# GELU of a state-space unit as one ScalarE activation instead of a five-step tanh form, in a Hymba block whose inverse square roots are powers on GpSimd

## The chip, the cores and the metric

One core of one Trainium2 chip runs the whole block. The time is the device time of one execution in microseconds (us). Two kernels are compared by the medians of their runs; the profile is of one more execution, whose own time is given beside its span.

## The reference

The input is 2048 positions of 1024 channels in float32; 16 learned meta tokens are put in front. One layer is computed:

```python
n1 = rmsnorm(h, norm1_g)
proj = n1 @ w_in                       # 1024 -> 1024
u = proj[..., :512]                    # 32 groups x 16 channels
v = proj[..., 512:]                    # 4 groups x 128 channels
# S5: 64 complex states a group, s[t] = a*s[t-1] + b u[t]
y = Re(C s) + d * u
g = jax.nn.gelu(y)                     # the tanh form
ys = g * sigmoid(g @ glu_w + glu_b)    # per group
# pooling: trailing means over 2, 4, 8, 16 positions minus v,
# then a 128x128 map per group
mixed = concat(rmsnorm(ys), rmsnorm(yp))
h = h + mixed @ w_out
ff = silu(n2 @ w_gate) * (n2 @ w_up)   # n2 = rmsnorm(h), 1024 -> 2816
h = h + ff @ w_down
out = rmsnorm(h)[16:]
```

The GELU is the step that the change touches; its tanh form is y/2 * (1 + tanh(0.798 * (y + 0.0447 y^3))).

## The kernel before

All large products are float32 by three matmuls on split operands: a high part h, rounded to the matmul's format, and the rest l, with hh + hl + lh (mm3, L119 to L121). So each weight and each activation that is multiplied is split first: the high part (names ending in h) on ScalarE (L112, or L115 with a scale), the low part (names ending in l) on VectorE (L87, or L96 with a scale).

The 2048 positions are cut into two halves, b = 0 and 1, of 1024: 128 chunks of T = 8 positions. The state space works on chunks: a unit is 4 of the 32 groups, so there are eight units a half, and ssm_unit(b, u) (L657 on) does one:

- pk, the unit's constants, comes by DMA (L661). For every second unit the projected input xu is turned to channel-major, by PE transposes into put (L669) and ScalarE copies to us (L670).
- pvs (L686, PE) is what the chunk adds to the state. VectorE rotates it (wr, tmp), scans it over the chunks (L691, z), and rotates back to st, with two products tmp on GpSimd; the step st<-st,tmp on VectorE is the last. In half 0 some small instructions on 128 x 4 elements (carry, sm) carry the state from half to half and start it from the meta tokens (pv, L677 and L678).
- py (PE, one bank of PSUM, 128 x 512): L700 is the part straight from us, L701 the part from the states st.
- The GELU of py goes to yview, which is the tile xu of that half. ScalarE squares py (L703), VectorE makes q = (q + 1) py, ScalarE the tanh (L705), and VectorE four times (q + 1) py, one instruction per group with a permuted write; all of VectorE's are the helper's line L96. The result is twice the GELU, and the factor is taken back later: in the tanh of the gate (L786, scale 0.25) and in the eps of the norm (L815, 16 EPS).

In time, the kernel runs through these stages. Up to 165 us are weights, parameters and the projection of half 0. Then the projection of half 1 (pj) runs on PE with the units of half 0 between its slices, to 296 us. In the transition, the eight tiles of w_out are loaded into two raw buffers (wraw) and split into wh and wl (load_w). The output stage then goes through eight position slots of half 0: out_pool transforms the pooled channels (pin, ppool), out_ssm turns g to position-major (pg, copied to gt, L780), multiplies by the gate's weights (pgate, L783), makes the gate with tanh (th, L786) and the product gt, and sums squares (sq, sqs on GpSimd); out_mm adds the norms' sums (pss, L812) and the output projection (po). Between the slots stand the units of half 1 and pool_block(1), which makes the trailing means with adds on GpSimd (sum), one VectorE instruction (pt) and a write to p_d1 by DMA. The output stage of half 1 follows to 560 us and the FFN after it.

The program is written in this order, but the order in which an engine's queue gets its instructions is chosen by a scheduler, at build time, from its own estimates of cost. At run time each engine runs its queue in that order; SyncE's queue issues the DMAs. PSUM tiles come from three pools; py, pvs and pv share the one with two buffers (ps_s).

Of the kernel before, what the change touches and what calls it, by code (L numbers as in the profile page):

```python
# [9 lines left out]
F32 = mybir.dt.float32  # L10
# [3 lines left out]
AF = mybir.ActivationFunctionType  # L14
ALU = mybir.AluOpType

P = 128
# [3 lines left out]
DSSM = 512  # L21
G = 32
H = 16
S = 64
T = 8
NB = 2
NCH = 128
UG = 4
# [1 line left out]
FF = 2816  # L30
NF = FF // P
EPS = 1e-6
GA = 0.7978845608028654
GC = math.sqrt(0.044715)
MAGIC = 12582912.0
PKN = 2568

# [2 lines left out]
def kernel(  # L40
# [54 lines left out]
    def stt(o, a, s, b, op0, op1):  # L95
        V.scalar_tensor_tensor(o, a, s, b, op0=op0, op1=op1)  # L96
# [560 lines left out]
    def ssm_unit(b, u):  # L657
        g0 = u * UG
        gs = slice(g0, g0 + UG)
        pk = ss_p.tile([P, PKN], F32, name="pk", tag="pk", bufs=2)  # L660
        SY.dma_start(pk, pk_d[u])  # L661
        pm, nm, mm = g4(pk[:, :512]), g4(pk[:, 512:1024]), g4(pk[:, 1024:1536])
        ct, sg = g4(pk[:, 1536:2052]), g4(pk[:, 2052:2568])
        if u % 2 == 0:
            us8[0] = ss_p.tile([P, 2 * UG, NCH], F32, name="us", tag="us", bufs=2)
            for h in range(2):
                pu = tr_tile("put")
                for i in range(UG):
                    PE.transpose(pu[:, i], xu[b][:, g0 + h * UG + i].rearrange("c t h -> c (t h)"), ident)  # L669
                A.copy(us8[0][:, h * UG:(h + 1) * UG], pu)  # L670
        us = us8[0][:, (u % 2) * UG:(u % 2 + 1) * UG]
        z = ss_p.tile([P, UG, NCH + 1], F32, name="z", tag="z", bufs=2)
        sm = ss_p.tile([P, 4, UG], F32, name="sm", tag="sm", bufs=2)
        if b == 0:
            pv0 = g4(s_tile("pv0"))
            for i in range(UG):
                PE.matmul(pv0[:, i, :2], pm[:, i], um_sb[:, g0 + i], start=True, stop=True)  # L677
            V.tensor_copy(sm[:, 2:4], pv0[:, :, :2].rearrange("p g c -> p c g"))  # L678
            rotate(sm[:, 0], sm[:, 1], sm[:, 2], ct[:, :, 1], sg[:, :, 1], 1)
            tt(sm[:, 0], sm[:, 0], r8[:, gs], M_)  # L680
            tt(z[:, :, 0], sm[:, 0], sm[:, 3], A_)
        else:
            V.tensor_copy(z[:, :, 0], carry[:, gs])
        pv = g4(s_tile("pvs"))
        for i in range(UG):
            PE.matmul(pv[:, i], pm[:, i], us[:, i], start=True, stop=True)  # L686
        wr = ss_p.tile([P, UG, NCH], F32, name="wr", tag="wr")
        tmp = ss_p.tile([P, UG, NCH], F32, name="tmp", tag="tmp", bufs=2)
        rotate(wr, tmp, pv, ct[:, :, 1:], sg[:, :, 1:], -1)
        for i in range(UG):  # L690
            V.tensor_tensor_scan(z[:, i, 1:], r8[:, g0 + i:g0 + i + 1].to_broadcast([P, NCH]), wr[:, i],  # L691
                                 z[:, i, 0:1], op0=M_, op1=A_)
        st = ss_p.tile([P, UG, NCH], F32, name="st", tag="st")
        tmp2 = ss_p.tile([P, UG, NCH], F32, name="tmp2", tag="tmp", bufs=2)
        rotate(st, tmp2, z[:, :, :NCH], ct[:, :, :NCH], sg[:, :, :NCH], 1, GP)
        if b == 0:
            rotate(carry[:, gs], sm[:, 1], z[:, :, NCH], ct[:, :, NCH], sg[:, :, NCH], 1)
        py = s_tile("py")
        for i in range(UG):
            PE.matmul(py[:, i * P:(i + 1) * P], us[:, i], mm[:, i], start=True, stop=False)  # L700
            PE.matmul(py[:, i * P:(i + 1) * P], st[:, i], nm[:, i], start=False, stop=True)  # L701
        q = ss_p.tile([P, UG * P], F32, name="q", tag="q")
        A.activation(q, py, AF.Square, scale=GC)  # L703
        stt(q, q, 1.0, py, A_, M_)
        A.activation(q, q, AF.Tanh, scale=GA)  # L705
        yv = yview(b)[:, u // 2]
        for i in range(UG):
            c0 = (u % 2 * UG + i) * H
            isl = slice(i * P, (i + 1) * P)
            stt(yv[:, :, c0:c0 + H], q[:, isl].rearrange("c (t h) -> c t h", h=H), 1.0,  # L710
                py[:, isl].rearrange("c (t h) -> c t h", h=H), A_, M_)

    def pool_block(b):
        vt = vts.pop(b)
# [59 lines left out]
    def out_ssm(b, t, mh, ml, sq):  # L774

        pt = tr_tile("pg")
        for k in range(4):
            PE.transpose(pt[:, k], yview(b)[:, k, t], ident)
        gt = wo_p.tile([P, 4, NCH], F32, name="gt", tag="gt")
        A.copy(gt, pt)  # L780
        pg = (s_tile if b else mm_tile)("pgate")
        for k in range(4):
            PE.matmul(pg[:, k * P:(k + 1) * P], glubd[:, k], gt[:, k], start=True, stop=True)  # L783
        th = wo_p.tile([P, 4, NCH], F32, name="th", tag="th")
        for k in range(4):
            A.activation(th[:, k], pg[:, k * P:(k + 1) * P], AF.Tanh, scale=0.25, bias=halfb[:, k:k + 1])  # L786
        fl = "p k c -> p (k c)"
        stt(gt.rearrange(fl), th.rearrange(fl), 1.0, gt.rearrange(fl), A_, M_)
        split(mh[:, :4], ml[:, :4], gt)
        A.activation(sq[:, 0], gt, AF.Square)  # L790
        tt(sq[:, :, :2], sq[:, :, :2], sq[:, :, 2:], A_, GP)
        sqs = wo_p.tile([P, 2, NCH], F32, name="sqs", tag="sqs", bufs=2)
        tt(sqs, sq[:, :, 0], sq[:, :, 1], A_, GP)
        return mh, ml, sqs
# [12 lines left out]
    def out_mm(b, t, mh, ml, sq, pooled=None):  # L807
        hx = hxs.pop((b, t))
        os = [None, pooled or out_half(mh, ml, 1)]
        pss = tr_tile("pss")  # L810
        for i in range(2):
            PE.matmul(pss[:, 0, i:i + 1], sq[:, i], ones, start=True, stop=True)  # L812
        rsp = small.tile([P, 2], F32, name="rsp", tag="rsp")
        rsqrt_into(rsp, pss[:, 0, :2], [2],
                   [((ALL[0], slice(0, 1)), 1.0 / DSSM, 16.0 * EPS),  # L815
                    ((ALL[0], slice(1, 2)), 1.0 / DSSM, EPS)])
        os[0] = out_half(mh, ml, 0)
        for q in (1, 0):
            for h in range(2):
                cs2 = slice(h * 512, (h + 1) * 512)  # L820
                stt(hx[:, cs2], os[q][h], rsp[:, q:q + 1], hx[:, cs2], M_, A_)
        for h in range(2):
            cs2 = slice(h * 512, (h + 1) * 512)
            jk = wo_p.tile([P, 4, NCH], F32, name="jk", tag="th")
            A.activation(jk.rearrange("p k c -> p (k c)"), hx[:, cs2], AF.Square, accum_out=ss2[:, h, b * T + t:b * T + t + 1])
        SY.dma_start(h2_d[b][t], hx)
        if t == T - 1:
            bs = slice(b * T, b * T + T)
            tt(ss2[:, 0, bs], ss2[:, 0, bs], ss2[:, 1, bs], A_)
            rsqrt_into(rs2[:, bs], ss2[:, 0, bs], [T], [(ALL, 1.0 / D, EPS)])  # L830
# [433 lines left out]
```

## Time and profile before

| what | value |
|---|---|
| median of three runs | 1892.83 us (1889.36 to 1895.19) |
| profiled execution, its own time | 1896.96 us |
| its span | 1895.2 us |
| TensorE busy | 1827.5 us |
| VectorE busy | 1250.3 us |
| GpSimd busy | 814.5 us |
| ScalarE busy | 681.9 us |

The span runs from the first to the last instruction of the profile; the rest of the execution's time lies around it. A row of a view names source line, engine, operation, and the tile written and the tiles read. PE is TensorE's matmuls, PEld its weight loads, DVE VectorE, ACT ScalarE, POOL GpSimd, SP SyncE. In brackets stands how long the engine was idle before the instruction and what ended that. Lines L87, L93, L96, L112 and L115 are those of helpers, and such rows are known by their tiles.

### The profile page before, as it was taken

Reading aid. Unit: us, or ns where it says so; the run is one execution under the profiler, and the core shown is the slowest. Engines: PE = TensorE matmul, PEld = TensorE weight load, DVE = VectorE, ACT = ScalarE, POOL = GpSimd, SP = SyncE. Lnnn points to the kernel's source line nnn. Section 1 sums busy time; section 2 is a strip of 40 time slices with the busy share of each in tenths; the row PEclk is TensorE's granted clock in tenths of the full one; section 3 lists DMA queues with packets and bytes.
Section 4 is the critical chain, followed back from the end, with each engine's and each line's share of the span. In section 5 each row is a group of like instructions: output and inputs, shape, how many; then the busy total and the mean of one; then the engine's idle time right before and its main releaser. Section 6 shows DMA issues by size and latency. Waiting matters only on the chain.

```text
span 1895.2 us, 23776 instructions
## 1 busy us (share of the span) xinstructions
PE 1827.5 (96%) x8497; PEld 1499.8 (79%) x8497; DVE 1250.3 (66%) x1993; ACT 681.9 (36%) x1228; POOL 814.5 (43%) x619
## 2 busy tenths in 40 slices
PE   7989996899999999999999999999999999999998
PEld 5867785788887788888887788888888888888886
DVE  5985878966456866666667866766666344435763
ACT  4332334343454333333335333233323343333441
POOL 1774424633244564554646866666562000003400
PEclk9999998899999999999999999999999999999999
DMA  6254425444355343543426654455447765536761
GB/s 181 69 176 164 137 92 172 172 156 137 102 177 162 114 159 106 169 139 125 156 95 202 200 197 139 156 170 172 130 150 228 213 202 177 153 102 208 249 215 71
DMA packets 260519, 298.38 MB, mean 157 GB/s; under 512 B 17148, under 2 KB 204048, under 8 KB 255536
## 3 DMA queue, kind: packets, MB, share of 16 engines
q1 hardware_dynamic: 260304, 296.84, 49.2%
q8 instruction: 67, 1.10, 0.2%
q14 instruction: 52, 0.43, 0.1%
q0 software_dynamic: 96, 0.01, 0.0%
HBM read 202.37 MB, written 96.53 MB: 158 GB/s over the span
## 4 chain that ended last, share of the span: by engine, by line
PE 73%; DVE 2%; DMA 2%; POOL 1%; ACT 1%; issue 1%; DVEq 0%; POOLq 0%; ACTq 0%
PE pr L119 14%; PE pr L120 14%; PE pr L121 14%; PE pd L119 8%; PE pd L120 7%; PE pd L121 7%; PE po L119 2%; PE po L121 2%; PE po L120 2%; DMA xp<-xr_d 1%; PE ptx L874 1%; PE pgate L783 1%; DMA hr<-h_d 1%; DVE wcl L87 1%; PE ppool L769 0%
## 5 line engine op out<-in xcount | busy, mean ns | idle before, releaser
L112 ACT CAST wch<-raw 128x512 fp32r<-128x512 f32 x176 | 108.6, 621 | 266.1 <-PE pr L120 240.0
L87 DVE TENSOR_TENSOR wcl<-raw,wch 128x512 fp32r<-128x512 f32 x176 | 178.0, 1014 | 37.7 <-ACT wch L112 36.7
L87 DVE TENSOR_TENSOR fl<-fr,fh 128x512 fp32r<-128x512 f32 x168 | 116.0, 702 | 127.5 <-ACT fh L112 120.7
L112 ACT CAST fh<-fr 128x512 fp32r<-128x512 f32 x168 | 96.5, 584 | 212.8 <-PE pd L120 180.0
L112 ACT CAST wch<-s 128x512 fp32r<-128x512 f32 x132 | 82.0, 622 | 228.2 <-PE pr L120 175.2
L87 POOL TENSOR_TENSOR s<-raw 128x512 f32<-128x512 f32 x44 | 67.7, 1540 | 173.3 <-DVE wcl L87 72.3
L87 DVE TENSOR_TENSOR wcl<-s,wch 128x512 fp32r<-128x512 f32 x132 | 117.6, 892 | 20.5 <-ACT wch L112 20.2
L87 POOL TENSOR_TENSOR db22h<-db22h,hd 128x512 f32<-128x512 f32 x4 | 5.2, 1291 | 256.4 <-DVE db22h L87 256.4
L87 POOL TENSOR_TENSOR rs<-rv,mhalf 128x1 f32<-128x1 f32 (+2 forms) x35 | 40.6, 1160 | 154.9 <-DVE rv L93 151.8
L119 PE MATMUL po<-wh,mh 128*128 128x512 f32 x256 | 104.4, 408 | 1.5 <-DVE hx L96 0.8
L119 PE MATMUL pj<-wh,xh 128*128 128x512 f32 x256 | 102.5, 408 | 3.2 <-ACT xh L112 2.3
L120 PE MATMUL pj<-wl,xh 128*128 128x512 f32 x256 | 102.9, 404 | 0.0
L121 PE MATMUL pj<-wh,xl 128*128 128x512 f32 x256 | 102.3, 405 | 0.0
L120 PE MATMUL po<-wl,mh 128*128 128x512 f32 x256 | 101.3, 396 | 0.0
L121 PE MATMUL po<-wh,ml 128*128 128x512 f32 x256 | 100.9, 395 | 0.0
L87 POOL TENSOR_TENSOR wr<-wr 128x512 f32<-128x512 f32 x44 | 67.3, 1530 | 72.9 <-DMA wr<-in_w_down_dram 67.8
L87 DVE TENSOR_TENSOR gt<-gt,ut 128x512 f32<-128x512 f32 x88 | 94.0, 1069 | 0.0
L87 POOL TENSOR_TENSOR tmp<-z,pk 64x512 f32<-64x512 f32 x32 | 49.7, 1553 | 84.3 <-issue 82.4
L87 DVE TENSOR_TENSOR gt<-pr,gt 128x512 f32<-128x512 f32 x66 | 45.4, 690 | 58.6 <-PE pr L121 58.4
L87 POOL TENSOR_TENSOR ut<-gt 128x512 f32<-128x512 f32 x22 | 33.4, 1520 | 107.7 <-DVE gt L87 107.7
L119 PE MATMUL pr<-xt2h,wch 128*128 128x512 f32 x176 | 69.9, 397 | 6.1 <-DVE gt L87 3.7
L1015 ACT ACTIVATE gt<-gt 128x512 f32<-128x512 f32 x88 | 55.5, 632 | 49.8 <-DVE gt L87 49.6
(394 smaller groups left out, 5611.2 us busy)
## 6 DMA issues: line engine op xcount, KB each, us to landing
fr<-ff_d SPq DMA_DIRECT2D x56, 704.0 KB, 5.0
raw<-in_w_gate_dram SPq DMA_DIRECT2D x44, 512.0 KB, 4.8
raw<-in_w_up_dram SPq DMA_DIRECT2D x44, 512.0 KB, 4.2
ff_d<-gt SPq DMA_DIRECT2D x22, 1024.0 KB, 3.9
pk<-pk_d SPq DMA_DIRECT2D x16, 1284.0 KB, 6.0
ff_d<-ut SPq DMA_DIRECT2D x22, 768.0 KB, 5.6
wr<-in_w_down_dram SPq DMA_DIRECT2D x22, 512.0 KB, 3.3
wd_d<-wr SPq DMA_DIRECT2D x22, 512.0 KB, 3.4
```

The source lines that it names most:

```text
L87: e.tensor_tensor(o, a, b, op=op)
L112: A.copy(hi, src)
L119: PE.matmul(o, lh, rh, start=first, stop=False)
L120: PE.matmul(o, lh, rl, start=False, stop=False)
L121: PE.matmul(o, ll, rh, start=False, stop=last)
L783: PE.matmul(pg[:, k * P:(k + 1) * P], glubd[:, k], gt[:, k], start=True, stop=True)
L874: PE.transpose(pt[:, k], r[:, (4 * h + k) * P:(4 * h + k + 1) * P], ident)
L1015: lambda i, j: A.activation(gt[:, i, j], gt[:, i, j], AF.Silu), b == 0 and f0 == 0)
```

## The change

The square, the two kinds of VectorE instruction and the tanh give way to one activation, Gelu_apprx_tanh, that reads py and writes yview permuted. Since the result is now the GELU and not twice it, the gate's tanh is scaled by 0.5 and the eps is 4 EPS.

```diff
@@ -30,8 +30,6 @@
 FF = 2816
 NF = FF // P
 EPS = 1e-6
-GA = 0.7978845608028654
-GC = math.sqrt(0.044715)
 MAGIC = 12582912.0
 PKN = 2568
 
@@ -699,16 +697,9 @@
         for i in range(UG):
             PE.matmul(py[:, i * P:(i + 1) * P], us[:, i], mm[:, i], start=True, stop=False)
             PE.matmul(py[:, i * P:(i + 1) * P], st[:, i], nm[:, i], start=False, stop=True)
-        q = ss_p.tile([P, UG * P], F32, name="q", tag="q")
-        A.activation(q, py, AF.Square, scale=GC)
-        stt(q, q, 1.0, py, A_, M_)
-        A.activation(q, q, AF.Tanh, scale=GA)
-        yv = yview(b)[:, u // 2]
-        for i in range(UG):
-            c0 = (u % 2 * UG + i) * H
-            isl = slice(i * P, (i + 1) * P)
-            stt(yv[:, :, c0:c0 + H], q[:, isl].rearrange("c (t h) -> c t h", h=H), 1.0,
-                py[:, isl].rearrange("c (t h) -> c t h", h=H), A_, M_)
+        c0 = u % 2 * UG * H
+        yv = yview(b)[:, u // 2][:, :, c0:c0 + UG * H].rearrange("c t (i h) -> c t i h", h=H)
+        A.activation(yv, py.rearrange("c (i t h) -> c t i h", i=UG, t=T), AF.Gelu_apprx_tanh)
 
     def pool_block(b):
         vt = vts.pop(b)
@@ -783,7 +774,7 @@
             PE.matmul(pg[:, k * P:(k + 1) * P], glubd[:, k], gt[:, k], start=True, stop=True)
         th = wo_p.tile([P, 4, NCH], F32, name="th", tag="th")
         for k in range(4):
-            A.activation(th[:, k], pg[:, k * P:(k + 1) * P], AF.Tanh, scale=0.25, bias=halfb[:, k:k + 1])
+            A.activation(th[:, k], pg[:, k * P:(k + 1) * P], AF.Tanh, scale=0.5, bias=halfb[:, k:k + 1])
         fl = "p k c -> p (k c)"
         stt(gt.rearrange(fl), th.rearrange(fl), 1.0, gt.rearrange(fl), A_, M_)
         split(mh[:, :4], ml[:, :4], gt)
@@ -812,7 +803,7 @@
             PE.matmul(pss[:, 0, i:i + 1], sq[:, i], ones, start=True, stop=True)
         rsp = small.tile([P, 2], F32, name="rsp", tag="rsp")
         rsqrt_into(rsp, pss[:, 0, :2], [2],
-                   [((ALL[0], slice(0, 1)), 1.0 / DSSM, 16.0 * EPS),
+                   [((ALL[0], slice(0, 1)), 1.0 / DSSM, 4.0 * EPS),
                     ((ALL[0], slice(1, 2)), 1.0 / DSSM, EPS)])
         os[0] = out_half(mh, ml, 0)
         for q in (1, 0):
```

Source lines after the change are 2 lower up to py and 9 lower from pool_block on: L703 and L705 are replaced by L702. On ScalarE there is one table load more than before, ahead of the first GELU; before, and after, one stands at the start and one at the FFN's first SiLU. The scheduler puts instructions in another order from the first GELU, about 186 us, to about 470 us; the rest of the queues, the FFN's among them, is as it was.

VectorE in the projection of half 1, around the end of unit (0,1): its rotation step is st<-st,tmp, and the instructions on 128x4 and 64x4 from sm on belong to the next unit. Before:

```order
L93 TENSOR_SCALAR rv<-ss 128x1
L678 COPY sm<-pv_2095 128x8
L87 TENSOR_TENSOR sm<-sm,pk 128x4
L87 TENSOR_TENSOR sm<-sm,pk 64x4 x2
L87 TENSOR_TENSOR sm<-sm 128x4
L87 TENSOR_TENSOR sm<-sm,r_156 128x4
L87 TENSOR_TENSOR z<-sm 128x4
L87 TENSOR_TENSOR st<-st,tmp_1968 128x512
```

and now:

```order
L85 TENSOR_TENSOR xl<-pt,xh 128x512
L91 TENSOR_SCALAR rv<-ss 128x1
L676 COPY sm<-pv_2081 128x8
L85 TENSOR_TENSOR st<-st,tmp_1961 128x512
L85 TENSOR_TENSOR sm<-sm,pk 128x4
L85 TENSOR_TENSOR sm<-sm,pk 64x4 x2
L85 TENSOR_TENSOR sm<-sm 128x4
L85 TENSOR_TENSOR sm<-sm,r_156 128x4
L85 TENSOR_TENSOR z<-sm 128x4
L94 SCALAR_TENSOR_TENSOR pt<-sum_1836,vt_495 128x8x128
L85 TENSOR_TENSOR wr<-pvs,pk 128x512
```

The step st<-st,tmp has moved ahead of the next unit's sm instructions, and pt of pool_block(0) now stands between these and that unit's wr.

VectorE at the end of the projection, around the end of unit (0,7); wl are splits of w_out, pt is of pool_block(1), wr and tmp from pvs are those of unit (1,0). Before:

```order
L87 TENSOR_TENSOR carry<-z,pk 128x4
L87 TENSOR_TENSOR sm<-z,pk 64x4 x2
L96 SCALAR_TENSOR_TENSOR wl_3003<-wraw,vcol,wh_3002 128x1024
L87 TENSOR_TENSOR carry<-carry,sm 128x4
L96 SCALAR_TENSOR_TENSOR wl_3009<-wraw,vcol,wh_3008 128x1024
L87 TENSOR_TENSOR st<-st,tmp_2852 128x512
L683 COPY z<-carry 128x4
L96 SCALAR_TENSOR_TENSOR wl_3015<-wraw,vcol,wh_3014 128x1024
L96 SCALAR_TENSOR_TENSOR q<-q,py 128x512
L96 SCALAR_TENSOR_TENSOR wl_3021<-wraw,vcol,wh_3020 128x1024
```

and now:

```order
L85 TENSOR_TENSOR sm<-z,pk 64x4 x2
L85 TENSOR_TENSOR carry<-carry,sm 128x4
L85 TENSOR_TENSOR st<-st,tmp_2803 128x512
L681 COPY z<-carry 128x4
L94 SCALAR_TENSOR_TENSOR wl_2947<-wraw,vcol,wh_2946 128x1024
L94 SCALAR_TENSOR_TENSOR wl_2953<-wraw,vcol,wh_2952 128x1024
L94 SCALAR_TENSOR_TENSOR wl_2959<-wraw,vcol,wh_2958 128x1024
L85 TENSOR_TENSOR wr<-pvs,pk 128x512
L85 TENSOR_TENSOR tmp<-pvs,pk 64x512 x2
L94 SCALAR_TENSOR_TENSOR pt<-sum_3107,vt_2031 128x8x128
L94 SCALAR_TENSOR_TENSOR wl_2965<-wraw,vcol,wh_2964 128x1024
```

The step st<-st,tmp has moved ahead of the first two splits, the third split has stayed ahead of unit (1,0)'s wr, and the two kinds of GELU instruction are gone. On PE, the matmuls that read this st (L701, now L699) have moved from behind the last matmul of the projection to sixteen matmuls ahead of it.

ScalarE at the same place; wh are the high parts of w_out, xu and vs the projected last slice, vt the transposed vs, us and gt copies of put and pg. Before:

```order
L219 ACTIVATE xu_160<-pj,rs 128x32x16
L226 ACTIVATE vs<-pj,rs 128x512
L115 ACTIVATE wh_3014<-wraw,vcol 128x1024
L703 ACTIVATE q<-py 128x512
L115 ACTIVATE wh_3020<-wraw,vcol 128x1024
L230 COPY vt_2045<-ptv 128x4x128
L705 ACTIVATE q<-q 128x512
L670 COPY us<-put 128x512 x2
L780 COPY gt<-pg 128x512
```

and now:

```order
L702 ACTIVATE xu_159<-py 128x8x64
L113 ACTIVATE wh_2952<-wraw,vcol 128x1024
L217 ACTIVATE xu_160<-pj,rs 128x32x16
L224 ACTIVATE vs<-pj,rs 128x512
L228 COPY vt_2031<-ptv 128x4x128
L771 COPY gt<-pg 128x512
L668 COPY us<-put 128x512
L113 ACTIVATE wh_2958<-wraw,vcol 128x1024
L668 COPY us<-put 128x512
L113 ACTIVATE wh_2964<-wraw,vcol 128x1024
```

The copy to vt has moved from behind the third and fourth of these wh to a place ahead of the third.

SyncE's queue issued the last six of w_out's eight tiles in three pairs, the second pair ahead of the first write of p_d1 and the third ahead of the second write. Now a pair and a single tile stand ahead of the first write of p_d1, a pair between the two writes, and the last tile behind the second.

## The prediction

> **What bounds the kernel now.** I read the page first: its first part (busy time by engine) and the slices.
>
> ```profile
> PE 1827.5 (96%) x8497; PEld 1499.8 (79%) x8497; DVE 1250.3 (66%) x1993; ACT 681.9 (36%) x1228; POOL 814.5 (43%) x619
> PE   7989996899999999999999999999999999999998
> PEclk9999998899999999999999999999999999999999
> ```
>
> TensorE is busy 96% of the span, and the change takes no matmul away. It can only shorten the time in which PE stands idle, or runs at a reduced granted clock. A slice is 47.4 us; besides the start, PE's digit falls in the seventh and eighth, at 284 to 379 us, and the clock with it. Next I asked for the stretches by engine (stretch and length; busy PE, PEld, DVE, ACT, POOL; granted clock; DMA share; GB/s).
>
> ```profile
> 165.00:460.00 295.00, 264.47 (x1503) 229.35 (x1502) 232.26 (x441) 106.33 (x209) 131.05 (x102) 0.95 0.40 137
> 296.00:336.00 40.00, 24.84 (x138) 22.13 (x139) 33.41 (x43) 16.23 (x27) 24.22 (x16) 0.79 0.55 177
> 313.00:336.00 23.00, 15.40 (x86) 13.91 (x86) 22.94 (x27) 9.21 (x17) 19.32 (x12) 0.78 0.41 125
> 560.00:1895.20 1335.20, 1319.11 (x5751) 1070.68 (x5749) 842.88 (x1101) 468.74 (x810) 567.35 (x389) 1.00 0.52 163
> ```
>
> From 560 us on is the FFN, whose order stays. The sixteen state-space units lie in 165 to 460 us, where PE idles 295.0 - 264.5 = 30.5 us. That is all the change can win there, beside the clock. Half of it, 40.0 - 24.8 = 15.2 us, lies in the 40 us between the projection and the full run of the output projection; I call it the transition. The waits of PE in 165 to 460 us name what ends them (total us, times, longest):
>
> ```profile
> PE py L701 <- DVE st L87: 12.0, 6, 3.0
> PE pss L812 <- POOL sqs L87: 4.7, 2, 3.8
> PE put L669 <- ACT vt L230: 2.9, 1, 2.9
> PE pvs L686 <- DVE sm L678: 2.5, 1, 2.5
> ```
>
> PE waits for st, the rotated states, which VectorE makes: for a VectorE queue that the GELU shares, not for the GELU itself. The timeline gives each wait its place (start, length, instruction, and in brackets the idle time before it):
>
> ```profile
> 183.42 0.49 PE L686 MATMUL pvs<-us,pk 128*128 128x128 f32 x2 [2.46 <-DVE sm L678]
> 185.24 0.63 PE L700 MATMUL py<-pk,us 128*128 128x128 f32 x2
> 206.63 0.49 PE L701 MATMUL py<-pk,st 128*128 128x128 f32 x2 [2.98 <-DVE st L87]
> 206.96 0.39 PE L700 MATMUL py<-pk,us 128*128 128x128 f32 x2
> 295.47 0.39 PE L121 MATMUL pj<-wh,xl 128*128 128x512 f32 x1
> 298.90 0.49 PE L701 MATMUL py<-pk,st 128*128 128x128 f32 x2 [3.04 <-DVE st L87]
> 304.44 1.12 PE L669 MATMUL put<-ident,xu 128*128 128x128 f32 x4 [2.95 <-ACT vt L230]
> 327.51 1.01 PE L812 MATMUL pss<-ones,sqs 128*128 128x1 f32 x4 [3.75 <-POOL sqs L87]
> 335.65 0.49 PE L119 MATMUL po<-wh,mh 128*128 128x512 f32 x1
> ```
>
> **Removed and added work.** The groups of instructions (busy total, mean ns of one, idle before):
>
> ```profile
> L703 ACT ACTIVATE q<-py 128x512 f32<-128x512 f32 x16 | 9.5, 591 | 35.4 <-PE py L701 32.9 <-issue 2.5
> L705 ACT ACTIVATE q<-q 128x512 f32<-128x512 f32 x16 | 10.1, 634 | 11.3 <-DVE q L96 11.2
> L96 DVE SCALAR_TENSOR_TENSOR q<-q,py 128x512 f32<-128x512 f32 x16 | 10.9, 684 | 10.2 <-ACT q L703 10.1
> L96 DVE SCALAR_TENSOR_TENSOR xu<-q,py 128x128 f32<-128x128 f32 x64 | 14.0, 279 | 2.2 <-ACT q L705 2.2
> L219 ACT ACTIVATE xu<-pj,rs 128x512 f32<-128x512 f32 x16 | 11.0, 687 | 16.3 <-PE pj L121 14.4 <-POOL ptp L87 1.8
> ```
>
> VectorE loses 10.9 + 14.0 = 24.9 us in 80 instructions, 1.56 us a unit; ScalarE loses 9.5 + 10.1 = 19.6 us. It gains sixteen GELUs that read py in PSUM and write permuted. No row shows one. Nearest are L703, the same read (591 ns), and L219, which reads PSUM and writes the same tile xu permuted (687 ns): 9.5 to 11.0 us in all. I take 0.6 us each, by L703, since in L219 the scale is a tile. Either way ScalarE ends 8.6 to 10.1 us lighter, at 36% busy, so the GELU itself is at nothing. If a reader of it came early, the price would be 0.1 us a unit. The new scales of L786 and the eps of L815 change no instruction: nothing.
>
> A table load is added at the first GELU. Its price is in the FFN's switch to SiLU:
>
> ```profile
> 598.07 1.28 ACT L1015 ACT_TABLE_LOAD   x1
> 599.37 0.63 ACT L1015 ACTIVATE gt<-gt 128x512 f32<-128x512 f32 x1
> 187.19 0.60 ACT L703 ACTIVATE q<-py 128x512 f32<-128x512 f32 x1 [11.49 <-PE py L701]
> ```
>
> From the load's start to the next ACTIVATE pass 1.30 us. The first GELU is where L703 stands at 187.19, and ScalarE idled 11.49 us in front of it: hidden. Without that cover it would cost 1.3. The Trainium skill (ScalarE: Activation LUTs, section "What ACT_TABLE_LOAD costs") counts 2.66 us for a switch, a load of 1283 ns and a drain of 1380 ns. The trace agrees on the load and shows no drain behind it; by the skill's figure the uncovered cost would be 2.7 instead of 1.3, and the sum the same.
>
> **Unit 1, the wait at 206.63.** VectorE's rows ahead of it:
>
> ```profile
> 204.78 1.20 DVE L87 TENSOR_TENSOR z<-sm 128x4 f32<-128x4 f32 x1
> 205.90 0.68 DVE L87 TENSOR_TENSOR st<-st,tmp 128x512 f32<-128x512 f32 x1
> ```
>
> The last rotation step of st stands behind the sm chain of unit 2, tiny instructions that the busy GpSimd stretches (1.20 us for 4 columns). In the new order it stands ahead of the chain, and PE loses the 2.98 us no more: bounds 0 to -3.0. What is late next: the chain is now followed by pt, which waits for a GpSimd sum, ahead of unit 2's wr, so unit 2 may be held. I give 1.0 back: -2.0. The 2.46 at 183.42 lies before the first changed VectorE instruction and stays.
>
> **The transition.** Before, two w_out splits stand ahead of st of unit (0,7); vt, the transposed v for which PE's put waits, stands on ScalarE behind splits that wait for a DMA.
>
> ```profile
> 296.97 1.28 DVE L96 SCALAR_TENSOR_TENSOR wl<-wraw,vcol,wh 128x1024 fp32r<-128x1024 f32 x1
> 298.16 0.68 DVE L87 TENSOR_TENSOR st<-st,tmp 128x512 f32<-128x512 f32 x1
> 302.77 1.15 ACT L115 ACTIVATE wh<-wraw,vcol 128x1024 fp32r<-128x1024 f32 x1 [0.83 <-DMA wraw<-in_w_out_dram]
> 303.83 0.56 ACT L230 COPY vt<-ptv 128x512 f32<-128x512 f32 x1
> 324.59 2.28 DVE L96 SCALAR_TENSOR_TENSOR wl<-wraw,vcol,wh 128x1024 fp32r<-128x1024 f32 x1
> 327.93 2.28 DVE L87 TENSOR_TENSOR st<-st,tmp 128x512 f32<-128x512 f32 x1
> 331.02 2.87 DVE L96 SCALAR_TENSOR_TENSOR wl<-wraw,vcol,wh 128x1024 fp32r<-128x1024 f32 x1
> ```
>
> After, st goes ahead of the splits and 2 x 1.28 = 2.6 us of them drop out of its chain, with 1.56 us of the previous unit's GELU; its matmuls move from behind the projection's last matmul to 16 ahead of it, so that these sixteen cover the rest. So the 3.04 goes. vt no longer follows the third and fourth wh: the 2.95 goes. Then the limit is the w_out splits. The last, 331.02 + 2.87 = 333.9, is followed by the po run at 335.65, 335.65 - 295.86 = 39.8 us after the projection's last matmul. VectorE's queue until 333.9 held 33.4 less about 2 us behind it, 31.4, and loses 1.56: last split at the earliest 30 us after. If nothing is stretched there (the last two splits took 2.28 and 2.87 instead of 1.28, the st at 327.93 took 2.28 instead of 0.68: 4.2 us), 26. With 2 us behind it, the po run starts 28 to 32 us after instead of 39.8: -7.8 to -11.8. I take the middle, -9.8, less 0.3 for the third split, which now stands ahead of unit (1,0)'s wr and needs a load: -9.5. It contains the 3.75 before pss and the reduced clock (0.79 over the stretch), not twice. The bound above is 0, if the splits' loads, not VectorE, set their end (rivals).
>
> **Later units.** Of the 12.0 us for st, 3.0 + 3.0 are spent above; the rest is partly in the transition. Out of the window's last 124 us I take -0.5 (0 to -4).
>
> Sum: -2.0 - 9.5 - 0.5 = -12.0. The profiled execution took 1896.96 us (span 1895.2), so 1885; it lies 4.1 above the median 1892.83, so **1881**.
>
> The Trainium skill (TensorE: Matmul & The Clock Gate, section "Part 1: The HAM clock gate") says that the clock halves after an idle window of about 3.4 us. Here pairs of matmuls took 0.63 us (185.24) behind the 2.46 us wait and 0.39 (206.96) behind the 2.98 one, so the trace does not follow the length of a single wait. Had the rule held at unit 1, its removed wait would win some 1.7 us more (an estimate from that page: 3.4 us at half clock); by the rows it wins nothing more.
>
> **The rivals.**
>
> *The waits come back elsewhere (no change).* The removed instructions all lie outside 313 to 336 us, where VectorE is busy 22.94 of 23.0; PE may just reach that block sooner and wait in it. For: that row. Against: st and vt feed the block. It gives -2.0 for unit 1 and -2 of the transition: 1889.
>
> *The loads become the bound (slower).* SyncE's queue now issues the last six raw tiles as two, one, two and one instead of in three pairs, the last one behind the second write of p_d1, which waits for VectorE's pt and GpSimd's sums. Three rounds become four.
>
> ```profile
> 297.00 1.60 SPq L204 DMA_DIRECT2D wraw<-in_w_out_dram  x2
> ```
>
> The other view, DMA issues (count, size, median us to landing):
>
> ```profile
> wraw<-in_w_out_dram SPq DMA_DIRECT2D x8, 512.0 KB, 3.3
> ```
>
> A round is landing 3.3 us, wh 1.15, wl 1.28 to 2.87, and the wait for the queue; before, three rounds took 333.9 - 297.0 = 36.9, 12.3 each. A fourth like them ends at +12.3; with unit 1's -2.0 that is +10.3: 1903. It decides from the point where the last split ends more than 38 us after the projection. Against: a bare round is 3.3 + 1.15 + 1.28 = 5.7, and four are 23 us.
>
> *The one activation is not one (no change to slower).* If the tables alternate between GELU and the gate's Tanh, eight units of half 1 bring 16 loads of 1.30: 20.8 us on ScalarE, at most all on the path from pgate to th, 1881 + 20.8 = 1902. The Trainium skill (ScalarE: Activation LUTs, section "Table sets: the hidden batching unit") tells to group functions by set, and lists gelu's set as separate from gelu_apprx_tanh. Against: the order holds one added load.
>
> *All waits go (faster).* PE's idle 30.5, less the 2.46 that stays and 3 of mixed small ones, is 25, and 1892.8 - 25 = 1868.
>
> **How the numbers follow.** Forecast (1875 to 1887) 0.61, all waits 0.08, no change 0.19, loads 0.10, tables 0.02. About 0.3% (5.7 us) can be told from no change: faster is below 1887.2, slower above 1898.5. Faster takes the forecast and all waits, 0.69; same 0.19; slower 0.12. The range reaches from 1868 to 1893, past the no-change case by its 4 us of spread, and leaves the loads and tables out.
>
> **What would show it.** Right: L702 at 0.6 to 0.7 us; no wait above 1 us for st near 205 us nor at the projection's end; no put wait for vt; the po run 27 to 32 us after the projection's last matmul; PE idle 18 to 20 us in 165 to 460. Wrong: that po run 38 us or more after it, wh waiting for wraw in front of it, or table loads between GELU and Tanh.

## The result, and the profile after

The changed kernel took 1885.98 us (median of 13 runs, 1882.54 to 1888.96); the kernel before, beside it, 1895.19 us (13 runs, 1889.07 to 1899.9). The ratio is 0.995, 95% interval 0.994 to 0.996: 9.2 us faster. The profiled execution took 1885.98 us, its span is 1884.2.

The page of the changed kernel, first part and slices:

```profile
PE 1822.9 (97%) x8497; PEld 1495.4 (79%) x8497; DVE 1232.4 (65%) x1913; ACT 673.8 (36%) x1213; POOL 816.9 (43%) x619
PE   7989997899999999999999999999999999999998
PEclk9999998999999999999999999999999999999999
```

PE's busy time itself fell by 4.6 us although it runs the same 8497 matmuls. VectorE lost 17.9 us, not 24.9: 7 us came back, since instructions that remain took longer.

The stage borders are read from PE's timeline: the first pv of half 0 (up to there the instructions are the same), the end of the projection's last matmul, and the first matmul of the FFN (pr; it starts at 587.99 us before and 577.91 after, so the output stage of half 1 reaches to there and not to 560 us). The stretches between them, as windows, first of before and then of after (stretch and length; busy PE, PEld, DVE, ACT, POOL; granted clock; DMA share; GB/s):

```profile
166.44:295.86 129.42, 123.06 (x706) 106.20 (x706) 105.44 (x229) 42.58 (x72) 52.06 (x42) 0.99 0.34 118
295.86:587.99 292.13, 265.82 (x1459) 229.11 (x1459) 193.29 (x317) 121.99 (x275) 125.25 (x102) 0.95 0.47 154
```

```profile
164.43:295.76 131.33, 125.12 (x720) 107.25 (x720) 99.89 (x198) 40.66 (x67) 51.15 (x42) 0.99 0.35 122
295.76:577.91 282.15, 259.67 (x1446) 222.97 (x1445) 182.28 (x267) 116.01 (x265) 129.32 (x102) 0.97 0.47 157
```

The projection has become 1.9 us longer, but it holds 14 more matmuls, which came forward from behind it; its idle time is 6.4 us before and 6.2 now. The stretch behind it is 10.0 us shorter: 3.8 us less idle (26.3 to 22.5) and 6.2 us less busy, 2.1 of them the matmuls that moved. So in the two stretches together idle time fell by 4.0 and busy time, at a higher granted clock (0.97 instead of 0.95 in the second), by 4.1.

The waits of PE in 165 to 460 us, after:

```profile
PE py L698 <- DVE tmp L85: 8.6, 1, 8.6
PE pvs L684 <- DVE sm L676: 5.8, 2, 3.4
PE pgate L774 <- ACT gt L771: 3.6, 4, 1.2
PE put L667 <- ACT gt L771: 3.5, 1, 3.5
PE py L699 <- DVE st L85: 1.2, 3, 0.8
PE put L667 <- ACT vt L228: 0.2, 1, 0.2
```

The 12.0 us for st are 1.2, and the 2.9 for vt are 0.2, as the order foretold. In their place the wait for tmp has grown from 2.1 us to 8.6, that of pvs from 2.5 to 5.8, and one of 3.5 for gt is new. The wait for tmp before:

```profile
PE py L700 <- DVE tmp L87: 2.1, 1, 2.1
```

In time (PE, after):

```profile
198.93 0.49 PE L699 MATMUL py<-pk,st 128*128 128x128 f32 x2 [0.25 <-DVE st L85]
213.65 1.35 PE L684 MATMUL pvs<-us,pk 128*128 128x128 f32 x8 [3.38 <-DVE sm L676]
295.37 0.39 PE L119 MATMUL pj<-wh,xl 128*128 128x512 f32 x1
297.93 1.15 PE L667 MATMUL put<-ident,xu 128*128 128x128 f32 x8 [0.24 <-ACT vt L228]
304.27 1.05 PE L774 MATMUL pgate<-gt,glubd 128*128 128x128 f32 x8
321.35 0.77 PE L698 MATMUL py<-pk,us 128*128 128x128 f32 x2 [8.59 <-DVE tmp L85]
323.35 2.08 PE L774 MATMUL pgate<-gt,glubd 128*128 128x128 f32 x8 [1.23 <-ACT gt L771]
328.45 0.48 PE L117 MATMUL po<-wh,mh 128*128 128x512 f32 x1
```

The last row is the start of the po run. VectorE's last split ends behind it, at 327.43 + 1.75 = 329.18:

```profile
327.43 1.75 DVE L94 SCALAR_TENSOR_TENSOR wl<-wraw,vcol,wh 128x1024 fp32r<-128x1024 f32 x1
```

The eight pgate matmuls of a slot take 1.05 us before the long wait and 2.08 behind it. The GELU itself, and its table load:

```profile
L702 ACT ACTIVATE xu<-py 128x512 f32<-128x512 f32 x16 | 9.4, 590 | 25.2 <-PE py L699 25.2
```

```profile
173.74 1.28 ACT L702 ACT_TABLE_LOAD   x1
183.93 0.60 ACT L702 ACTIVATE xu<-py 128x512 f32<-128x512 f32 x1 [8.91 <-PE py L699]
```

590 ns, at the low end of the bounds, permuted write or not; the load lies in ScalarE's idle time, and there is no other between GELU and tanh.

### The profile page after: what moved, and what is told of

It reads as the page before. It is cut to its first block, busy times and chain, and to the rows that moved or that the text cites. A ratio compares the mean times of both kernels' runs of the same rounds, so it can differ in the third digit from the quotient of the medians.

```text
span 1884.2 us, 23676 instructions
## 1 busy us (share of the span) xinstructions
PE 1822.9 (97%) x8497; PEld 1495.4 (79%) x8497; DVE 1232.4 (65%) x1913; ACT 673.8 (36%) x1213; POOL 816.9 (43%) x619
## 4 chain that ended last, share of the span: by engine, by line
PE 73%; DVE 3%; DMA 2%; POOL 1%; issue 1%; ACT 1%; DVEq 0%; POOLq 0%; ACTq 0%
PE pr L117 14%; PE pr L118 14%; PE pr L119 14%; PE pd L117 8%; PE pd L118 8%; PE pd L119 8%; PE po L117 2%; PE po L119 2%; PE po L118 2%; DVE wcl L85 1%; PE pgate L774 1%; DMA hr<-h_d 1%; PE ptx L865 1%; DMA xp<-xr_d 0%; PE ppool L760 0%
## 5 line engine op out<-in xcount | busy, mean ns | idle before, releaser
L85 POOL TENSOR_TENSOR rs<-rv,mhalf 128x1 f32<-128x1 f32 (+2 forms) x35 | 31.5, 900 | 154.1 <-DVE rv L91 144.8
```

The source lines that it names most:

```text
L85: e.tensor_tensor(o, a, b, op=op)
```

## The experiments

Theory A: the gain is VectorE's queue, lighter and in another order. Its rival, theory B: the gain is the shorter way from py to the GELU. A second rival within A: the order alone, not the work. Each time is the median beside runs of the kernel before on the same chip; "faster" and "slower" are against those.

**One half at a time.** One half takes the one activation and the other keeps the five steps (here half 0; in the other kernel b == 1):

```diff
+        if b == 0:
+            c0 = u % 2 * UG * H
+            yv = yview(b)[:, u // 2][:, :, c0:c0 + UG * H].rearrange("c t (i h) -> c t i h", h=H)
+            A.activation(yv, py.rearrange("c (i t h) -> c t i h", i=UG, t=T), AF.Gelu_apprx_tanh)
+            return
         q = ss_p.tile([P, UG * P], F32, name="q", tag="q")
```

> Only the units of half 0 take the one activation; those of half 1 keep the five-step form (and their doubled result). Its queues stand as after the change up to the end of the projection, st of unit (0,7) ahead of the w_out splits. Theory A (the gain comes from VectorE's queue: less work, and st and vt ahead of the splits at the transition): most of the gain of 9.2 us is here, 5 to 8 us faster than before, since the transition starts like that of the changed kernel, and the later units keep their 1.56 us of VectorE each. Theory B (the gain is the shorter way from py to the GELU, which only half 1 shows to a waiting reader, pg to th): within 2 us of before.

> Only the units of half 1 take the one activation. The queues stand as before the change up to the end of the projection, the first two w_out splits ahead of st of unit (0,7). Theory A: 1 to 4 us faster than before (the 3 us of the later units, none of the 3.04 for st). Theory B: 6 to 9 us faster. If the two halves' gains add up to about 9 us, they are separate; if they give more than 11 or less than 7 together, the schedule's order mixes them.

Half 0 alone: 1890.81 against 1896.01, ratio 0.9973 (0.9962 to 0.9984). Half 1 alone: 1890.83, ratio 0.9969 (0.9956 to 0.9981). Each is 5.2 us faster. The sum, 10.4, fits the 9.2 of both, so nothing speaks for a mixing of the halves; but each gain is known only to about 2 us either way. Half 0 is as theory A had it and speaks against B; half 1 brings more than A gave it (1 to 4 us) and less than B (6 to 9). The half-0 kernel has the waits of the changed one up to the transition, the 8.6 us one included (8.60); the half-1 kernel still has 3.04 us for st there. Where the half-1 kernel gains, its profiled execution does not show: the two stretches take 131.3 and 292.3 us there, no less than before, since a lower granted clock takes back the idle time that went. The 40 us behind its projection:

```profile
291.82:331.82 40.00, 27.25 (x134) 24.82 (x134) 33.45 (x43) 16.18 (x26) 24.53 (x16) 0.70 0.53 175
```

134 matmul records took 27.25 us at a clock of 0.70, where before 137 took 24.70 at 0.79: less idle, and nothing gained in this one execution.

**Work put back.** In front of the GELU, five instructions of the old shapes on a scratch tile:

```diff
+        sf = st.rearrange("p g c -> p (g c)")
+        stt(q, sf, 1.0, sf, A_, M_)
+        for i in range(UG):
+            isl = slice(i * P, (i + 1) * P)
+            stt(q[:, isl], sf[:, isl], 1.0, sf[:, isl], A_, M_)
```

> The changed kernel with the removed VectorE work put back as work for nothing: five instructions a unit of the old shapes, from st into a scratch tile that nobody reads. The GELU stays one activation, and st of unit (0,1) and of unit (0,7) stand where the change put them. Theory A with the work as its main part: the gain is gone for the most part, 0 to 3 us faster than before. Theory A with the order as its main part: 5 to 8 us faster. Theory B (the shorter way): 8 to 10 us faster, as the changed kernel.

1900.88 against 1896.01: 4.9 us slower, ratio 1.0028 (1.0019 to 1.0037). That is beyond every expectation. The GELU is that of the changed kernel, and so is the place of st of units (0,1) and (0,7), and it is some 14 us slower than that: more work on VectorE costs time. But this run puts back more than the change took away. Its 80 instructions are busy 22.5 + 12.9 = 35.4 us (411 and 808 ns each) where the removed ones took 24.9 (279 and 684 ns), so VectorE has 309.4 us of work in the two stretches, against 298.7 before; and the scheduler moved other instructions of the queues too, among them the sixth and the eighth split and st of unit (1,0). So it does not price the work that the change removed. Against theory B it says little, since the added work could hide such a gain; what speaks against B is that no wait of PE before the change, in 165 to 595 us, is put down to an output of the GELU. The part behind the projection is as long as before:

```profile
299.70:591.82 292.12, 265.40 (x1446) 226.53 (x1445) 193.23 (x307) 115.94 (x265) 135.03 (x102) 0.96 0.46 152
```

**The order alone.** The kernel before, all its work kept:

```diff
-    woh, wol = load_w(w_out[0], lambda k: col("sng", k) if k < 4 else col("png", k - 4),
+    with tc.issue_after(us8['st'].ins):
+      woh, wol = load_w(w_out[0], lambda k: col("sng", k) if k < 4 else col("png", k - 4),
```

(us8['st'] is the last st<-st,tmp so far, that of unit (0,7); issue_after makes the block's instructions stand behind it in its engine's queue.)

> The kernel before with its five-step GELU; only VectorE's w_out splits are held behind st of unit (0,7), as in the changed kernel. Order alone: the wait of 3.04 us for st at the end of the projection goes, and if the transition was set by when st came, 3 to 6 us faster. If the transition is set by the sum of VectorE's work until the last split (31 us, unchanged here): within 2 us of before, the wait coming back in front of the po run.

1884.69 against 1896.01: 11.3 us faster, ratio 0.9937 (0.9923 to 0.995), more than either expectation gave. A change of order alone, without any GELU change, brings as much as the change. It was asked for by one edge, but the scheduler moved more in answer: the second pvs behind the projection, for one, starts 11.3 us after the projection's last matmul instead of 18.8. Its windows row from the projection's last matmul to the FFN:

```profile
289.96:571.05 281.09, 261.32 (x1458) 224.28 (x1459) 194.44 (x316) 122.17 (x275) 128.53 (x102) 0.98 0.49 161
```

281.1 us, against 292.1; and its last split ends 42 us after the projection (332.13 - 289.96), later than before (38.0) and than after the change (33.4), and PE waits 1.07 us for it. So a stage can become shorter though its last split ends later: that end alone does not set it. (This profiled execution, 1878.67 us, is the fastest of the five.)

**The same program again.**

> The kernel before once more, unchanged, for its stages: the profiled executions so far differ by up to 6 us in the first 165 us, where all have the same instructions. If that is chance of an execution, this one starts anywhere from 160.5 to 166.5 us, with the same 129.4 us for the projection and about 292 us from the projection's last matmul to the FFN's first, and its time is that of before within 0.3%. If it belongs to the program, it starts at 166.4 again.

1896.26 against 1895.17, ratio 1.0006 (0.9993 to 1.0019). Its start took 163.8 us where the first execution took 166.4, with the same instructions: chance. Its projection took 129.5 and the rest, up to the FFN, 290.8:

```profile
293.23:584.05 290.82, 264.84 (x1459) 228.48 (x1459) 192.84 (x317) 121.67 (x275) 125.44 (x102) 0.96 0.46 155
```

The stage behind the projection so differs by 1.3 us between two executions of one program, and by 2.4 between two with the same queues (the changed kernel and gelu_other_set, below); smaller differences of one profile say nothing. The projection can differ as much: half1_only, with the queues of before up to its end, takes 131.3 us for it instead of 129.4, and unit_first, with those of the changed kernel, 133.3 instead of 131.3, at granted clocks of 0.97 and 0.96 instead of 0.99. Their idle times differ by less than 0.3 us, so idle time is the steadier measure.

**ScalarE's side.**

```diff
         A.activation(yv, py.rearrange("c (i t h) -> c t i h", i=UG, t=T), AF.Gelu_apprx_tanh)
+        A.activation(q, py, AF.Gelu_apprx_tanh)
```

> The changed kernel with each GELU run twice, the second from py into a scratch tile that nobody reads: 16 more activations of 0.6 us, 9.4 us of ScalarE in all, 0.6 us longer until py is free. If the GELU lies beside other work as predicted (ScalarE 36% busy): within 3 us of the changed kernel, so 6 to 12 us faster than before. If ScalarE's queue is on the path in the units, 9 us of it come back: no change from before.

1885.29 against 1895.17, ratio 0.9956 (0.9942 to 0.9971): like the changed kernel. 9.5 us more of ScalarE cost nothing, as the prediction had it.

```diff
-        A.activation(yv, py.rearrange("c (i t h) -> c t i h", i=UG, t=T), AF.Gelu_apprx_tanh)
+        A.activation(yv, py.rearrange("c (i t h) -> c t i h", i=UG, t=T), AF.Gelu)
```

> The changed kernel with the function Gelu (by the error function, so slightly other values) in place of Gelu_apprx_tanh; its set of tables is not that of the gate's tanh. If each change of set is a load of 1.3 us and the loads stand between units and slots of half 1: up to 16 loads more, 20.8 us of ScalarE, and 5 to 20 us slower than the changed kernel (4 us faster to 11 us slower than before). If ScalarE hides them: within 3 us of the changed kernel. If the function shares the set: the same queues and the same time as the changed kernel.

1886.04 against 1895.17, ratio 0.9958 (0.9943 to 0.9973), and a single table load ahead of the first GELU, as in the changed kernel. I had taken the tables of Gelu for another set than tanh's; with one load for all units and slots, tanh shares a set with that function too, so this run does not price an alternation. The price of 16 loads stays untried. Since VectorE's order is that of the changed kernel, it serves as its second execution: idle 28.8 us in the two stretches against 28.7, busy 387.1 against 384.8.

**The new wait in front of pvs.**

```diff
-                    tt(nxt[:, :, 2:], cur[:, :, 2:], cur[:, :, 1:N2 - 1], A_, GP)
+                    tt(nxt[:, :, 2:], cur[:, :, 2:], cur[:, :, 1:N2 - 1], A_, GP if b else V)
```

> The changed kernel with the last of pool_block(0)'s sums on VectorE instead of GpSimd (half 0 only). That sum ended at 204.5 us and held VectorE 1.98 us in front of pt and unit (0,2), which PE paid with 3.38 us in front of pvs. If that chain is the cause: the wait in front of pvs falls below 1 us, the projection stage takes 128 to 130 us instead of 131.3, and the kernel is 2 to 4 us faster than the changed one (11 to 14 us faster than before). If it is not: the wait stays at 3 us. Then, or if the later queues change for the worse, within 2 us of the changed kernel.

1886.74 against 1895.17, ratio 0.9959 (0.9946 to 0.9972): no better than the changed kernel, and the wait is still 2.95 us. The projection did take 129.0 us, as the first case expected, but only 0.4 of the 2.3 us are idle time; the rest is busy time, in which executions of one order differ as much. The stretch behind it took 287.8 us. The chain in the changed kernel, PE's pvs of unit (0,2) and then VectorE's rows:

```profile
201.97 1.06 PE L684 MATMUL pvs<-us,pk 128*128 128x128 f32 x8
```

```profile
204.49 1.23 DVE L94 SCALAR_TENSOR_TENSOR pt<-sum,vt 128x1024 f32<-128x1024 f32 x1 [1.98 <-POOL sum L85]
205.63 0.68 DVE L85 TENSOR_TENSOR wr<-pvs,pk 128x512 f32<-128x512 f32 x1
212.08 1.31 DVE L85 TENSOR_TENSOR sm<-z,pk 64x4 f32<-64x4 f32 x2
213.43 0.17 DVE L676 COPY sm<-pv 128x8 f32<-128x8 f32 x1
```

The copy that ends PE's wait takes 0.17 us and stands behind the whole chain of unit (0,2). It frees one of the two PSUM buffers of ps_s. That chain could have begun when pvs was done, at 203.03; behind the wait for the sum and pt it began at 205.63, 2.6 us later. The edit put 1.23 us of VectorE's own work in the place of 1.98 us of waiting, and pt stayed: the chain still began 1.9 us late (204.35 against 202.46). So the 0.4 us that the wait lost are what this edit can show; it does not clear pt and the sum as the cause.

**Both helpful edits.** before_st_first, with the one activation in half 1:

> The two edits that helped apart, together: the one activation in half 1 alone (5.2 us faster than before), and the w_out splits held behind st of unit (0,7) (11.3 us). Half 0 keeps the five-step form and its order. If the first works on the later units and the second on the transition, they add: 14 to 18 us faster than before, 5 to 9 us faster than the changed kernel. If both take away the same idle time: 10 to 12 us faster than before. Below 8 us the gain of either was an accident of its own order.

1881.35 against 1893.37, ratio 0.9941 (0.9928 to 0.9955): 12.0 us. They do not add: of the 5.2 us, 0.7 are left, and the idle time is that of before_st_first (26.8 and 26.2 us). Both seem to take the same idle time.

**What bounds the transition now.** Three edits of the changed kernel. The unit written first:

```diff
+    ssm_unit(1, 0)
     woh, wol = load_w(w_out[0], lambda k: col("sng", k) if k < 4 else col("png", k - 4),
...
     pool1 = pool_block(1)
-    ssm_unit(1, 0)
```

> The changed kernel with unit (1,0) written ahead of the w_out loads in the program, so that the scheduler puts its wr and tmp ahead of the third split and tmp of unit (1,1) further ahead. If the 8.59 us that PE waits for that tmp come from the splits put in front of the units: that wait falls below 4 us, the stretch from the projection's last matmul to the FFN's first is 274 to 280 us instead of 282, and the kernel is 2 to 8 us faster than the changed one. If the sum of VectorE's work up to the last split is the bound: within 2 us of the changed kernel, the wait only changing place.

No loads of the last six tiles (late is true for w_out):

```diff
+            if late and n >= 2:
+                raw = raws[n % 2]
+            else:
+                SY.dma_start(raw, w[k * P:(k + 1) * P, :])
```

> The changed kernel without the loads of the last six w_out tiles: the first two raw tiles are split over and over, so ScalarE and VectorE do the same number of splits and never wait for a transfer. If the loads bound the transition: it shortens by the waits of wh for wraw, and the kernel is 4 to 8 us faster than the changed one. If VectorE's work is the bound, within 2 us of it; slower is possible, since splits that are ready early are put ahead of the units.

No sums in the first two steps of pool_block(1):

```diff
-            for s in (1, 2, 4, 8)[:k + 1]:
+            for s in (1, 2, 4, 8)[:0 if b and k < 2 else k + 1]:
```

> The changed kernel without the sums of the first two steps of pool_block(1) (six GpSimd adds, 8 us of GpSimd in the transition; pt is made from vt alone). If VectorE's work in the transition is stretched by GpSimd: splits and st there take 1.3 and 0.7 us instead of 1.4 to 2.3, the last split ends 4 to 6 us earlier, and the kernel is 3 to 6 us faster than the changed one. If the order alone bounds it: within 2 us of the changed kernel.

unit_first: 1878.7 against 1893.37, ratio 0.9925 (0.9909 to 0.994), 14.7 us faster, some 5 better than the changed kernel: the fastest here that leaves nothing out. The wait for tmp fell from 8.59 to 5.33 us, less than I expected, yet idle time behind the projection is 17.8 us instead of 22.5, although PE now waits 3.29 us for the last split:

```profile
297.11:574.11 277.00, 259.20 (x1445) 222.33 (x1445) 182.58 (x267) 116.82 (x265) 126.74 (x102) 0.98 0.48 160
```

no_late_loads: 1871.64, ratio 0.9883 (0.986 to 0.9906), 21.7 us faster and 12 better than the changed kernel, above the range for "the loads bound it":

```profile
296.01:564.46 268.45, 256.09 (x1445) 220.66 (x1445) 169.62 (x263) 110.92 (x260) 124.73 (x102) 0.99 0.47 154
```

Idle time is 12.4 us there. But this run takes away two things at once. With no transfer to wait for, the scheduler also put the splits earlier: six of the eight end before the projection's last matmul, where two did, and VectorE's work behind it is 169.6 us instead of 182.3. So the run fits a bound by the loads and one by VectorE's work alike. In the changed kernel the loads show as waits of ScalarE's wh and VectorE's wl, not of PE:

```profile
305.32 1.15 ACT L113 ACTIVATE wh<-wraw,vcol 128x1024 fp32r<-128x1024 f32 x1 [2.14 <-DMA wraw<-in_w_out_dram]
310.60 1.15 ACT L113 ACTIVATE wh<-wraw,vcol 128x1024 fp32r<-128x1024 f32 x1 [2.61 <-DMA wraw<-in_w_out_dram]
```

```profile
300.64 1.28 DVE L94 SCALAR_TENSOR_TENSOR wl<-wraw,vcol,wh 128x1024 fp32r<-128x1024 f32 x1 [5.12 <-ACT wh L113]
```

no_sums: 1882.82, ratio 0.9937 (0.9915 to 0.9958), 10.6 us faster, hardly more than the changed kernel. The splits do become short, but the wait for tmp stays and the last split ends later (332.98 against 329.18):

```profile
320.54 1.28 DVE L94 SCALAR_TENSOR_TENSOR wl<-wraw,vcol,wh 128x1024 fp32r<-128x1024 f32 x1
331.71 1.27 DVE L94 SCALAR_TENSOR_TENSOR wl<-wraw,vcol,wh 128x1024 fp32r<-128x1024 f32 x1
```

```profile
320.66 0.77 PE L698 MATMUL py<-pk,us 128*128 128x128 f32 x2 [8.74 <-DVE tmp L85]
```

This run does not take the stretching away, though. GpSimd's sums of the third step came forward, and GpSimd is busy 14.9 of the 24.9 us from the projection's last matmul to that wait's end, against 16.3 of 25.6 in the changed kernel. What the splits won, the scan lost (no_sums first, then the changed kernel):

```profile
308.32 5.62 DVE L689 TENSOR_TENSOR_SCAN z<-r,z,wr 128x128 f32<-128x128 f32 x4
```

```profile
312.13 2.08 DVE L689 TENSOR_TENSOR_SCAN z<-r,z,wr 128x128 f32<-128x128 f32 x4
```

So whether GpSimd's stretching of VectorE, on which the prediction's bounds leaned, binds the transition stays untested.

**All runs on one scale.** Idle time is the length of the two stretches less PE's busy time in them (before: 129.42 + 292.13 - 123.06 - 265.82 = 32.7), from each profiled execution; the last column is the difference of the medians.

| kernel | PE idle, us | PE busy, us | against before, us |
|---|---|---|---|
| before, twice | 32.7, 32.3 | 388.9, 387.9 | 0 |
| changed | 28.7 | 384.8 | -9.2 |
| gelu_other_set | 28.8 | 387.1 | -9.1 |
| two_gelus | 29.4 | 387.9 | -9.9 |
| sum8_on_vector | 29.7 | 387.1 | -8.4 |
| half0_only | 30.5 | 387.7 | -5.2 |
| half1_only | 29.4 | 394.3 | -5.2 |
| dummy_work | 34.7 | 393.1 | +4.9 |
| before_st_first | 26.2 | 384.4 | -11.3 |
| half1_st_first | 26.8 | 387.0 | -12.0 |
| unit_first | 23.8 | 386.5 | -14.7 |
| no_sums | 25.7 | 384.9 | -10.6 |
| no_late_loads | 18.2 | 382.1 | -21.7 |

The times follow the idle times, though not strictly (half1_only and two_gelus have the same idle time and are 4.7 us apart). Against the 32.5 us of before, each us of idle time goes with 1.5 to 3.2 us of time; where much idle time went, 1.5 to 2.1. Part of the excess is busy time, which is lower in most kernels that idle less. The rest is not explained; one profiled execution stands here beside a median of several, and before_st_first's, for one, was 6.0 us below its median.

## Why the prediction was right, and where it was not

- **The sign and the size.** Forecast: 12.0 us less; measured: 9.2. Faster, and in the range. The stages account for part of that only: over the two executions of each order, the two stretches became 6.2 us shorter.
- **The GELU at nothing.** Right: 590 ns, in idle time, and a second one costs nothing. So does the table load, 1.28 us in ScalarE's idle time.
- **Unit 1, -2.0.** The wait for st went (2.98 to 0.25), but the 1.0 that I gave back was mis-sized: 3.38 us came back one unit later, in front of pvs. The projection's idle time fell by 0.15 us. The holder that I named, pt and GpSimd's sum ahead of unit (0,2)'s wr, is there and delays that unit by 2.6 us; that it causes the wait is not shown.
- **The transition, -9.5.** The waits for st and vt went, and the po run began 32.7 us after the projection's last matmul (328.45 - 295.76) instead of 39.8: -7.1, outside -7.8 to -11.8 by 0.7. The step that failed is "then the limit is the w_out splits", set by the sum of VectorE's work. The po run did not wait for the last split: it began 0.7 us before that ended, and before_st_first is faster with a later last split. The sum was mis-sized, too. It counted VectorE's busy time up to the last split (31.4 us) and put its idle time at nothing; that was 6.6 us before (31.4 busy of 38.0) and 5.0 after (28.4 of 33.4), so the last split came 33.4 us after the projection and not 26 to 30. Nearly all of the 5.0 is one wait, 5.12 us in front of the third split (300.64), whose load was issued at 292.58 and whose wh could start at 299.46; I had given 0.3 for it. What bounds the rest of the transition stays open. unit_first shows that the order in front of the units is part of it (5.5 us better than the changed kernel); no_late_loads points to the raw tiles, two at a time, but also moved VectorE's work; and VectorE was busy 20.6 of the 25.6 us up to the end of PE's wait for tmp.
- **Later units, -0.5.** Mis-sized: behind the po run's start another 2.9 us were won (10.0 - 7.1), within the bound of 4 given. Their waits for st (2.45 and 1.68 us before) fell below 0.8.
- **The clock.** I added nothing for it, beyond the stretch. The two executions of each order give a mean busy time of 388.4 us before and 385.9 after: some 2.5 us, beside 3.8 of idle time; but the two of the changed order differ by 2.3 from each other. I took PE idle time of 18 to 20 us in 165 to 460 as the mark of being right; it is 295.0 - 269.1 = 25.9 (before 30.5). So the number came out by two errors that offset each other, too much idle time removed and no clock: that the forecast lies so near is luck in part. Behind the wait of 8.59 us the granted clock was 0.50 (323.35 to 325.40), and eight pgate matmuls took 2.08 us instead of 1.05; before the change it was 0.64 behind the wait of 2.46 us (183.42 to 187.00), where the pairs took 0.63 us instead of 0.39, and 1.00 behind the one of 2.98. The Trainium skill (TensorE: Matmul & The Clock Gate, section "Part 1: The HAM clock gate") has the clock halved after an idle window of about 3.4 us. The trace agrees for the long wait, and differs for the one of 2.46 us.
- **The rivals.** "The waits come back elsewhere" was half true and deserved more than 0.19: the three waits that went at the two places were 8.5 us (2.7, 3.0 and 2.7), and the idle time that went was 4.0. "The loads become the bound" may have named the right resource, but not its sign: four rounds were not longer than three had been (last split 33.4 us after the projection, before 38.0). Of the signs of being wrong, one came: wh waited 2.14 and 2.61 us for wraw ahead of the po run. No run showed the tables alternating. "All waits go" was far off.

What stays open: the change removes VectorE work and reorders four queues. The new place of st with all the old work wins 11.3 us, so the order alone can bring the gain. Whether the removed work brings any of it, no run shows, since dummy_work puts back 10.5 us more than was removed. How the 9.2 us divide between the two is not settled. Of the 11.0 us between the two profiled spans, 2.0 lie before the first changed instruction and 0.9 in the FFN, where nothing changed; that part is chance.

## What to carry to other kernels

Where a scheduler orders the queues, an edit is a new order first and less work second: compare the orders, and try the order alone, since one edge may bring as much as the edit. A wait that goes is only won if nothing stands late behind it, so price a removal by the idle time of the whole stage, not by the wait's row. When work is put back as a control, measure what it takes: the same shapes took 35.4 us here instead of 24.9. And in these runs less idle time on TensorE went with more than its length in time, 1.5 us or more for each us; the granted clock is part of that, and the rest is not explained.

## What was not expected of the hardware

The first 165 us, with the same instructions in all kernels, took 160.5 to 166.4 us in the profiled executions. A function of another name, Gelu, needed no more table loads beside tanh than Gelu_apprx_tanh did (one). And a VectorE instruction on 128 x 4 elements takes 0.15 to 0.17 us while GpSimd is idle, but often 1.2 and up to 1.8 us while it is busy; yet the run without the first two steps' sums did not show what that costs: GpSimd stayed nearly as busy there, and one scan took 5.62 us instead of 2.08.
